# Last tile's operands in three pieces, the first block's norms by halves, and its second-half weights loaded ahead of the merge factors

## The chip, the cores and the metric

The kernel runs on one core of a Trainium2 chip. The metric is the device time of one execution in microseconds (us); three executions are timed and their median is given. One further execution is recorded by the hardware profiler, and every view below is of that one.

## What is computed

One layer of a hybrid decoder for a prompt of 2048 positions and a group of 32 sample rows, in f32:

```python
def _layer_prompt(x, biases, norm1_g, w_in, sgu_ln_g, sgu_ln_b, sgu_w, sgu_b, w_out,
                  norm2_g, w_gate, w_up, w_down):
    q, k, v, u, vg = _project(x, norm1_g, w_in)          # RMSNorm, then one projection
    ...
    att = _merge_branches(outs, lses).reshape(B, S, D_ATT).astype(x.dtype)
    ...
    x = x + jnp.concatenate([att, u * gate], axis=-1) @ w_out
    x = x + _swiglu(x, norm2_g, w_gate, w_up, w_down)
    ...

def _swiglu(x, g, w_gate, w_up, w_down):
    h = _rmsnorm(x, g)
    return (jax.nn.silu(h @ w_gate) * (h @ w_up)) @ w_down
```

D_MODEL is 1024, there are 8 attention heads of 64, and D_FF is 2816, which is 22 slices of 128. After the layer a final RMSNorm gives the result. The change is in the part from the output projection (`w_out`) to the first products with `w_gate` and `w_up`.

## The kernel before

The kernel is one program in four stages: the input projection and the gating unit; attention, head by head; then, for three **blocks** of token tiles (tiles of 128 tokens: 6, 6, and 4 with the sample rows beside them), the output projection with the second norm; and the SwiGLU products of that block. Each operand of a matmul is held as a high and a low part, and each product is three matmuls (high by high, high by low, low by high). The instructions of every engine are issued in the order in which the code is run, so each engine works through its own list in that order and waits at its head. SyncE (SP) issues nearly all DMAs, also in order.

Order in time is written with a clock of **ticks**. `tick()` advances it and runs what `later(n, fn)` has put down for that tick, and only then the matmuls that follow are issued. With `ahead=True` an entry goes before the others of its tick. A tick lies before every four slices of the output projection (12 matmuls) and before every product.

**First block, first half of the columns.** Tile 0 has its first 512 output columns in a PSUM bank already when the block begins. `open_unit` computes those of tiles 1 to 5, in ticks 1 to 10, each into its own bank, by `B.banks = (2, 0, 3, 4, 5, 2)`: tile 5 takes the bank of tile 0 again. `open_end` (an addition on DVE, L1422) empties a bank into the residual `acc`. Between these, `split_cat` makes the high and low parts of the next tile's input. The merged attention of the last head for positions 1024 to 2047 is made here too: `last_half` weights are turned and stored to `f_d` (`turn`, `store`), loaded back spread over the partitions (`merge_load`), multiplied in on POOL (`merge`, in `rest`, L1084 to L1088), and stored to `cat_d` by `merge_store`. The merged values stand in the tiles `obs[h]` (ring `ob`, two buffers) and `o3s[h]` (ring `wide`, two buffers).

**Second half.** `half1_load` loads the eight slices of `w_out` for columns 512 to 1023 into the ring `fraw` (eight buffers), `half1_split` makes their parts: high on ACT, low on POOL (L138). The parts go, two slices at a time, into `wide` (slices 0, 1 and 4, 5; named `woh`) and `ob` (slices 2, 3 and 6, 7; named `wol`), in place of the tiles of heads 6 and 7. `second_phase` then computes the six tiles' second halves and weaves the norms in by `norm2_slot`: slot k ends tile k-1 (`out_end`), sums its squares on ACT, takes the root and its reciprocal, scales it (`norm2_scale`), and turns tile k-2 into operands (`Operands`: 8 transposes on PE, then `first`, `second`, `third`, `last` on ACT, DVE and POOL). In blocks 2 and 3 `first_end` has ended the first half early and summed its squares (`norm2_half`), so that the slot sums 512 columns; in block 1 the slot sums all 1024.

**Products.** `one(u, q)` issues the products q = 0 to 6 of a **unit**, which is one slice of D_FF for some tiles of the block; a product is 12 matmuls into one of four PSUM banks taken in turn. The first slice is cut into two units: tiles 0 to 3 and 4 to 5 in blocks 1 and 2 (256 and 128 columns), two tiles each in block 3 (136 columns each). Before the first product stands slot n, and before product 4 slot n+1, which makes the last tile's operands whole: all of its ACT, DVE and POOL work is issued there. The bank of product 3 is read on DVE in product 4's turn (L1682), and the first product of the second unit, the eighth, takes that bank again. In product 2 the gate's silu runs on ACT (L1701).

Of the kernel before, what the change touches and what calls it, by code (L numbers as in the profile page):

```python
# [65 lines left out]
def hymba_step(ctx: ExitStack, tc: tile.TileContext, A: dict, O: dict):  # L66
# [99 lines left out]
    def zn_tile():  # L166
        return rp.tile([P, 512], F32, name="zn", tag="zn", bufs=3)
# [7 lines left out]
    def raw_tile():  # L175
        return rp.tile([P, 512], F32, name="raw", tag="raw", bufs=RAW)
# [891 lines left out]
    def merge_load(h, ch):  # L1068

        if h < H - 2:  # L1070
            f = pair_tile(F32)
            mf[h, ch] = (f[:, 0], f[:, 1])
            sync.dma_start(f, dap(f_d, h * 2 * T + ch * 512, [[0, P], [T, 2], [1, 512]]))
            return
        mf[h, ch] = (raw_tile(), zn_tile()) if h < H - 1 else (fraw(), fraw())
        for z, t_ in enumerate(mf[h, ch]):
            sync.dma_start(t_, dap(f_d, (h * 2 + z) * T + ch * 512, [[0, P], [1, 512]]))

# [24 lines left out]
    def merge_store(h, c0, c1):  # L1103
        for z in range(2):
            r0 = DA * (z + 1) + h * C
            sync.dma_start(cat_d[r0:r0 + C, c0 * 512:c1 * 512], obs[h][z * C:(z + 1) * C, c0 * 512:c1 * 512])
# [175 lines left out]
    def fraw():  # L1282
        return pool_["fw"].tile([P, 512], F32, name="fr", tag="fr", bufs=8)
# [32 lines left out]
    def later(n, fn, *args, ahead=False):  # L1316
        due[clock[0] + n, not ahead, len(seq)] = (fn, args)
        seq.append(0)

    def tick():  # L1320
        clock[0] += 1
        while due and min(due)[0] <= clock[0]:
            fn, args = due.pop(min(due))
            fn(*args)
# [40 lines left out]
    def split_wo(B, half, s, place, eng_lo=None):  # L1365
        B.wo[half, s] = wh, wl = place(s)
        split_sb(wh, wl, raws.pop(("o", half, s)), eng_lo=eng_lo)
# [69 lines left out]
        newton(r, v)  # L1437
        return r

    def norm2_half(B, i):  # L1440

        B.s1[i] = s1 = fl.tile([P, 4], F32, name="s1", tag="s1", bufs=6)
        act.activation(zn_tile(), B.acc[i][:, 0:512], AF.Square, accum_out=s1[:, 0:1])

    def norm2_square(B, i, junk):

# [204 lines left out]
    def product(B, u, q):  # L1651

        f, a, b = u["f"], u["a"], u["b"]
        n = (b - a) * B.w
        ps = ps_m()[:, 0:n]
        wh, wl = ops[f, q]
        xh, xl = (x[:, a:b, TOK[q]] for x in B.ops)
        out = ps.rearrange("p (i w) -> p i w", w=B.w)
        for k in range(4):
            ks = slice(k * P, (k + 1) * P)  # L1660
            pe.matmul(out, wh[:, ks], xh[:, :, k], start=(k == 0), stop=False)  # L1661
            pe.matmul(out, wh[:, ks], xl[:, :, k], start=False, stop=False)  # L1662
            pe.matmul(out, wl[:, ks], xh[:, :, k], start=False, stop=(k == 3))  # L1663

        rings = ((raw_tile, raw_tile, raw_tile, zn_tile), (zn_tile, zn_tile, zn_tile, raw_tile), (zn_tile, raw_tile, zn_tile, raw_tile))[min(u["n"], 2)]
        if q in (0, 1, 3, 4):
            v = (0, 1, None, 2, 3)[q]
            u["t", v] = rings[v]()[:, 0:n]
        c11, c21, c12, c22 = (u.get(("t", v)) for v in range(4))
        if q == 0:  # L1670
            act.activation(c11, ps, AF.Copy)
        elif q == 1:
            dve.tensor_add(c21, c11, ps)
        elif q == 2:
            dve.tensor_add(c11, c11, ps)
            u["g", 0] = silu_of(u, 0, c11)
        elif q == 3:
            dve.tensor_add(c12, c21, ps)
            u["s1"] = ps
        elif q == 4:  # L1680
            dve.tensor_add(c21, c21, ps)
            dve.tensor_add(c22, c21, u["s1"])  # L1682
        elif q == 5:
            dve.tensor_add(c12, c12, ps)  # L1684
            u["g", 1] = silu_of(u, 1, c12)
        elif q == 6:
            if a == 0:
                B.h[f % FC] = wide_pair("hw") + (hs4[:, f // FC % 2 * FC + f % FC] if B.last else None,)
            lows = hidden(B, u, 1, c22)
            dve.tensor_add(c21, c21, ps)  # L1690
            lows += hidden(B, u, 0, c21)
            for args in lows:
                if f + 1 < NF:
                    later(1, dve.tensor_sub, *args)
                else:
                    dve.tensor_sub(*args)

    def silu_of(u, z, c):

        g = bank(z)[:, 0:c.shape[-1]] if u["f"] else c  # L1700
        act.activation(g, c, AF.Silu)  # L1701
        return g
# [106 lines left out]
    def open_end(B, i):  # L1809
        out_end(B, i, 0, B.open.pop(i))  # L1810
# [39 lines left out]
        for fn, *args in what:  # L1850
            fn(*args)

    def half1_split(B, *ss):
        for s in ss:
            split_wo(B, 1, s, half1_place)

    def half1_load(*ss):
        for s in ss:
            load_wo(1, s, fraw)
# [22 lines left out]
    def second_phase(B, order, after=None):  # L1882

        for k, i in enumerate(order):
            norm2_slot(B, k, order)
            B.half1[i] = ps = ps_o()
            for c in range(2):
                tick()
                out_part(B, i, 1, range(c * 4, c * 4 + 4), ps, c == 0, c == 1)
            if after:  # L1890
                after(i)
        later(1, norm2_slot, B, len(order), order, ahead=True)
        later(5, norm2_slot, B, len(order) + 1, order, ahead=True)

    def first_block(B):

        for i in (1, 2):
            load_cat(B, i, 0, KD, acc_place(2 * i))
        plan.run(10 ** 9)
        split_cat(B, 1)  # L1900
        split_cat(B, 2)
        B.place()
        load_cat(B, 3, 0, KD)
        merge_store(h, 1, 2)
        load_acc(B, 1)
        load_acc(B, 0)
        load_cat(B, 4, 0, KD)
        load_cat(B, 5, 0, KD)
        merge_store(h - 1, 2, 4)
        half1_load(*range(4))  # L1910

        def rest():
            for ch in (2, 3):
                merge(h, ch, pool)
            merge_store(h, 2, 4)
            half1_load(*range(4, KD))
            sync.dma_start(gain[0], dap(A["final_g"], 0, [[0, P], [1, D]]))

        w = last_half["w"]
        for n, what in ((2, [(w.turn, lambda: ps_t(1)), (w.store, zn_tile), (split_cat, B, 3)]),  # L1920
                        (3, [(merge_load, h, 2), (merge_load, h, 3)]),
                        (4, [(split_cat, B, 4), (rest,)]), (5, [(open_end, B, 1)]),
                        (6, [(half1_split, B, 0, 1), (split_cat, B, 5)]), (7, [(open_end, B, 0)]),
                        (8, [(half1_split, B, 2, 3)]), (9, [(half1_split, B, 4, 5), (sources, B, 0, 0, 1, 2, 3)]),
                        (10, [(half1_split, B, 6, 7)]), (11, [(sources, B, 1, 0, 1, 2, 3)])):
            later(n, both, *what)
        for i in (1, 2):
            open_unit(B, i)
        for i in (3, 4, 5):
            open_unit(B, i)  # L1930
        first_operands(B)

        def more_acc(i):
            if i in (1, 2):
                load_acc(B, 2 * i)
                load_acc(B, 2 * i + 1)

        second_phase(B, range(6), more_acc)
# [6 lines left out]
    def next_block(B, downs, finals):  # L1945

        n = len(B.rows)
        order = [n - 1] * B.last + list(range(B.nt))
        B.banks = {i: y for y, i in enumerate(order)}
        B.place()  # L1950
        tiles = [i for i in order if B.rows[i] == P]
        skip = n - len(tiles)
        for j, i in enumerate(tiles):
            if j < 3:
                load_cat(B, i, 0, KD)
            else:
                later(2 * j - 5, load_cat, B, i, 0, KD)
            later(3 + 2 * (j + skip), split_cat, B, i)
        half1_load(*range(4))
        later(3, half1_load, *range(4, KD))  # L1960
        for s in (6, 7):
            later(s - 5, split_wo, B, 0, s, lambda s: op_tile())
        for y, fn in enumerate(finals):
            later(2 + 2 * y, fn)
        for y, i in enumerate(order):
            later(12 + 2 * y, first_end, B, i)
        for y in range(4):
            later(8 + (2 if B.last else 3) * y, half1_split, B, 2 * y, 2 * y + 1)
            later(10 + 3 * y, sources, B, 0, *((2 * y, 2 * y + 1) if y < 3 else (6,)))
        for fn in downs:  # L1970
            fn()
        for i in order:
            open_unit(B, i)
        first_operands(B)
        second_phase(B, order)
# [193 lines left out]
```

## Time and profile before

| | us |
|---|---|
| time, median of 3 executions (lowest to highest) | 2611.22 (2607.18 to 2616.19) |
| the profiled execution's own time | 2606.15 |
| its span, first to last instruction | 2604.4 |
| PE busy with matmuls, share of the span | 2484.0, 95% |
| DVE, ACT, POOL busy | 1411.0, 1220.7, 1373.8 |
| mean granted TensorE clock | 0.979 |

The mean granted clock is the share of full speed that PE was given; a stage with 0.50 does half as much in the same time while PE counts as fully busy. Block 1's part from its first `open_unit` to its first product runs from 941.46 to 1018.47 us of the span; the corresponding first products of blocks 2 and 3 begin at 1620.42 and 2190.95.

### The profile page before, as it was taken

The page shows a single profiled execution, that of the slowest core. Times are in us where ns is not written, and L with a number is a line of the kernel's source. Part 1 is how long each engine was busy: PE and PEld are TensorE (multiplying, and loading weights), DVE is VectorE, ACT ScalarE, POOL GpSimd, SP SyncE. Part 2 cuts the span into 40 slices and gives each one's busy share as a digit, 9 for nine tenths or more (in the row PEclk, how much of TensorE's full clock was granted, in tenths as well). Part 3 has the DMA queues.
Part 4 walks back from the last instruction along what each step waited for, and adds up shares of the span by engine and source line. Part 5 has one row for each costly group of instructions (what it writes and reads, how often), then busy time and mean ns, then how long its engine had stood idle before and what let it go on. Part 6 is the DMA issues. An engine that isn't in the chain of part 4 may idle for free. (4 is left out here: it accounts for less than half of the span.)

```text
span 2604.4 us, 38948 instructions
## 1 busy us (share of the span) xinstructions
PE 2484.0 (95%) x13598; PEld 2192.0 (84%) x13598; DVE 1411.0 (54%) x2772; ACT 1220.7 (47%) x2567; POOL 1373.8 (53%) x1074
## 2 busy tenths in 40 slices
PE   8998899999999889999999999999999999999997
PEld 6777687677988777988989988999999987999996
DVE  3359686345888856444444465444444466444445
ACT  6423334446877746554554545332323335444332
POOL 2035754123576656775766743563544534666663
PEclk9999999999999999999999999999999998999998
DMA  7764853578687664464553564464554643555553
GB/s 244 223 204 146 279 152 126 180 249 271 185 231 222 170 191 159 154 201 143 177 183 129 195 184 144 170 208 156 174 186 147 209 156 118 206 197 199 198 196 110
DMA packets 313408, 479.99 MB, mean 184 GB/s; under 512 B 25841, under 2 KB 178834, under 8 KB 307326
## 3 DMA queue, kind: packets, MB, share of 16 engines
q1 hardware_dynamic: 307740, 468.48, 55.9%
q10 hardware_dynamic: 5474, 9.04, 1.2%
q8 instruction: 108, 1.77, 0.3%
q14 instruction: 86, 0.70, 0.1%
HBM read 381.72 MB, written 165.83 MB: 210 GB/s over the span
## 5 line engine op out<-in xcount | busy, mean ns | idle before, releaser
L1604 POOL TENSOR_TENSOR op<-fr,op 128x512 fp32r<-128x512 f32 x385 | 488.7, 1299 | 299.1 <-ACT op L1600 279.1
L1661 PE MATMUL ps_m<-xh,op 128*128 128x384 f32 (+4 forms) x1932 | 618.6, 320 | 3.7 <-DVE zn L1682 3.7
L1663 PE MATMUL ps_m<-xh,op 128*128 128x384 f32 (+4 forms) x1932 | 618.1, 320 | 0.0
L1662 PE MATMUL ps_m<-xl,op 128*128 128x384 f32 (+4 forms) x1932 | 617.2, 319 | 0.0
L1734 PE MATMUL ps_o<-dw,hw 128*128 128x512 f32 x2040 | 484.0, 392 | 13.1 <-DVE acc L1736 13.1
L1734 PEld LDWEIGHTS ps_o<-dw,hw 128*128 128x128 f32 x2040 | 379.6, 188 | 95.9 <-DVE acc L1736 19.8
L1661 PEld LDWEIGHTS ps_m<-xh,op 128*128 128x128 f32 x1932 | 371.8, 192 | 8.3 <-issue 2.7
L1662 PEld LDWEIGHTS ps_m<-xl,op 128*128 128x128 f32 x1932 | 371.6, 192 | 3.5
L1663 PEld LDWEIGHTS ps_m<-xh,op 128*128 128x128 f32 x1932 | 371.6, 192 | 0.0
L1736 DVE TENSOR_TENSOR acc<-acc,ps_o 128x512 f32<-128x512 f32 (+1 forms) x362 | 247.1, 687 | 213.7 <-PE ps_o L1734 213.7
L1701 ACT ACTIVATE ps_t<-zn 128x384 f32<-128x384 f32 (+1 forms) x126 | 58.3, 463 | 474.0 <-DVE zn L1684 367.8
L1600 ACT ACTIVATE op<-fr 128x512 fp32r<-128x512 f32 x396 | 235.3, 623 | 22.2 <-DMA fr<-ab_d 14.9
L138 POOL TENSOR_TENSOR dw<-fd,dw 128x1024 fp32r<-128x1024 f32 x66 | 158.7, 2405 | 122.1 <-ACT dw L135 122.1
L318 PE MATMUL ps_s<-wh,xh 128*128 128x512 f32 x480 | 197.9, 412 | 6.5 <-ACT xh L135 5.9
L319 PE MATMUL ps_s<-wl,xh 128*128 128x512 f32 x480 | 192.4, 401 | 1.0 <-DVE wl L226 1.0
L320 PE MATMUL ps_s<-wh,xl 128*128 128x512 f32 x480 | 191.6, 399 | 0.0
L1604 POOL TENSOR_TENSOR op<-pair,op 128x512 fp32r<-128x512 f32 x63 | 81.5, 1302 | 117.1 <-ACT op L1600 117.1
L1711 ACT ACTIVATE hw<-ps_t 128x384 fp32r<-128x384 f32 (+1 forms) x126 | 56.0, 453 | 175.3 <-DVE ps_t L1707 174.4
L318 PEld LDWEIGHTS ps_s<-wh,xh 128*128 128x128 f32 x480 | 93.0, 194 | 36.4 <-issue 8.3
L320 PEld LDWEIGHTS ps_s<-wh,xl 128*128 128x128 f32 x480 | 92.8, 193 | 20.6 <-DVE xl L138 0.3
L319 PEld LDWEIGHTS ps_s<-wl,xh 128*128 128x128 f32 x480 | 93.1, 194 | 19.7 <-DVE wl L226 2.2
L611 POOL TENSOR_TENSOR vl<-kv,vh 100x512 fp32r<-100x512 f32 (+1 forms) x32 | 46.0, 1438 | 109.9 <-ACT vh L605 43.9
(484 smaller groups left out, 4776.1 us busy)
## 6 DMA issues: line engine op xcount, KB each, us to landing
fr<-ab_d SPq DMA_DIRECT2D x308, 256.0 KB
fd<-in_w_down_dram SPq DMA_DIRECT2D x66, 512.0 KB
out_ks_dram<-in_cache_k_dram SPq DMA_DIRECT2D x56, 512.0 KB
out_vs_dram<-in_cache_v_dram SPq DMA_DIRECT2D x56, 512.0 KB
ab_d<-fr SPq DMA_DIRECT2D x88, 256.0 KB
raw<-in_w_in_dram SPq DMA_DIRECT2D x72, 256.0 KB
qk_d<-pair SPq DMA_DIRECT2D x64, 256.0 KB
ab_d<-pair SPq DMA_DIRECT2D x63, 256.0 KB
```

The costliest lines, as they stand in the source:

```text
L138: (eng_lo or pool).tensor_sub(lo, src, hi.bitcast(F32))
L318: pe.matmul(o[j], xh[:, k, :], wh, start=(k == 0), stop=False)
L319: pe.matmul(o[j], xh[:, k, :], wl, start=False, stop=False)
L320: pe.matmul(o[j], xl[:, k, :], wh, start=False, stop=(k == KD - 1))
L1600: act.activation(ops[f, j][0], ab[f][j], AF.Copy)
L1604: (pool if f or j in POOL_LOW else dve).tensor_sub(lo_, ab[f][j], hi.bitcast(F32))
L1661: pe.matmul(out, wh[:, ks], xh[:, :, k], start=(k == 0), stop=False)
L1662: pe.matmul(out, wh[:, ks], xl[:, :, k], start=False, stop=False)
L1663: pe.matmul(out, wl[:, ks], xh[:, :, k], start=False, stop=(k == 3))
L1701: act.activation(g, c, AF.Silu)
L1734: pe.matmul(ps[0:nr], l_, r_[:, cs], start=(z == 0 and y == 0), stop=(z == FC - 1 and y == len(pairs) - 1))
L1736: dve.tensor_add(B.acc[i][0:nr, cs], B.acc[i][0:nr, cs], ps[0:nr])
```

## The change

1. **Last tile.** Slot n+1 is replaced by three entries: `Operands` and `first` before product 4, `second` before product 5, `third` and `last` before product 6, in every block. The silu of the first unit's product 2 is issued three ticks later, before product 5 and after `second`.
2. **Norms.** In block 1 the first halves of tiles 0 and 1 are ended and their squares summed in ticks 9 and 7 (`first_half`), where only `open_end` ran in ticks 7 and 5; those of tiles 3 to 5 are ended before the second four slices of their own second half. Tile 2 stays as it was. A square root on one column is issued in tick 10 (`root_ahead`).
3. **Loads.** The merge factors are loaded in tick 2 instead of 3, into `zn` tiles and one `raw` tile instead of four of `fraw`; the storing of head 6's merged values, which stood ahead of tick 1, is issued after them; slices 4 to 7 of the weights are loaded in tick 2 instead of after the last merge's store. `turn` and `store` move from tick 2 to 1.
4. **Splits.** The weights' parts are made in ticks 5, 6, 8 and 9 (were 6, 8, 9 and 10), and the low parts of all slices but 4 and 5 are made on DVE instead of POOL.

```diff
-        mf[h, ch] = (raw_tile(), zn_tile()) if h < H - 1 else (fraw(), fraw())
+        mf[h, ch] = (raw_tile() if h < H - 1 or ch > 2 else zn_tile(), zn_tile())
...
-    def norm2_half(B, i):
+    def norm2_half(B, i, junk=None):
...
-        act.activation(zn_tile(), B.acc[i][:, 0:512], AF.Square, accum_out=s1[:, 0:1])
+        act.activation(zn_tile() if junk is None else junk, B.acc[i][:, 0:512], AF.Square, accum_out=s1[:, 0:1])
...
-            u["g", 0] = silu_of(u, 0, c11)
+
+            def gate():
+                u["g", 0] = silu_of(u, 0, c11)
+
+            if b < B.nt:
+                later(3, gate, ahead=True)
+            else:
+                gate()
...
-    def half1_split(B, *ss):
+    def half1_split(B, eng_lo, *ss):
         for s in ss:
-            split_wo(B, 1, s, half1_place)
+            split_wo(B, 1, s, half1_place, eng_lo)
...
                 tick()
+                if c and k > 2 and i in B.open:
+                    first_end(B, i)
                 out_part(B, i, 1, range(c * 4, c * 4 + 4), ps, c == 0, c == 1)
...
-        later(5, norm2_slot, B, len(order) + 1, order, ahead=True)
+        last = {}
+
+        def last_operands(*steps):
+            if not last:
+                last["x"] = Operands(B, order[-1])
+            for step in steps:
+                getattr(last["x"], step)()
+
+        for n, steps in ((5, ("first",)), (6, ("second",)), (7, ("third", "last"))):
+            later(n, last_operands, *steps, ahead=True)
...
         load_cat(B, 5, 0, KD)
-        merge_store(h - 1, 2, 4)
         half1_load(*range(4))
+
+        def factors():
+            for ch in (2, 3):
+                merge_load(h, ch)
+            merge_store(h - 1, 2, 4)
+            half1_load(*range(4, KD))
 
         def rest():
             for ch in (2, 3):
                 merge(h, ch, pool)
             merge_store(h, 2, 4)
-            half1_load(*range(4, KD))
             sync.dma_start(gain[0], dap(A["final_g"], 0, [[0, P], [1, D]]))
 
+        def first_half(i):
+            open_end(B, i)
+            norm2_half(B, i, B.X[0][:, i, 0:512])
+
+        def root_ahead():
+            t_ = fl.tile([P, 4], F32, name="s1", tag="s1", bufs=6)
+            act.activation(t_[:, 0:1], ident[:, 0:1], AF.Sqrt)
+
         w = last_half["w"]
-        for n, what in ((2, [(w.turn, lambda: ps_t(1)), (w.store, zn_tile), (split_cat, B, 3)]),
-                        (3, [(merge_load, h, 2), (merge_load, h, 3)]),
-                        (4, [(split_cat, B, 4), (rest,)]), (5, [(open_end, B, 1)]),
-                        (6, [(half1_split, B, 0, 1), (split_cat, B, 5)]), (7, [(open_end, B, 0)]),
-                        (8, [(half1_split, B, 2, 3)]), (9, [(half1_split, B, 4, 5), (sources, B, 0, 0, 1, 2, 3)]),
-                        (10, [(half1_split, B, 6, 7)]), (11, [(sources, B, 1, 0, 1, 2, 3)])):
+        for n, what in ((1, [(w.turn, lambda: ps_t(1)), (w.store, zn_tile)]), (2, [(split_cat, B, 3), (factors,)]),
+                        (4, [(split_cat, B, 4), (rest,)]), (5, [(half1_split, B, dve, 0, 1)]),
+                        (6, [(half1_split, B, dve, 2, 3), (split_cat, B, 5)]), (7, [(first_half, 1)]), (8, [(half1_split, B, None, 4, 5)]),
+                        (9, [(half1_split, B, dve, 6, 7), (first_half, 0), (sources, B, 0, 0, 1, 2, 3)]),
+                        (10, [(root_ahead,)]), (11, [(sources, B, 1, 0, 1, 2, 3)])):
             later(n, both, *what)
```

In blocks 2 and 3 the call `half1_split` now passes `None`, which keeps POOL for the low part.

More of the change, by code (lines that the diff above doesn't have):

```diff
@@ L1967, in next_block @@
         for y in range(4):
-            later(8 + (2 if B.last else 3) * y, half1_split, B, 2 * y, 2 * y + 1)
+            later(8 + (2 if B.last else 3) * y, half1_split, B, None, 2 * y, 2 * y + 1)
             later(10 + 3 * y, sources, B, 0, *((2 * y, 2 * y + 1) if y < 3 else (6,)))
```

## The prediction

> **What bounds the kernel now.** PE does, by the page's first part:
>
> ```profile
> PE 2484.0 (95%) x13598; PEld 2192.0 (84%) x13598; DVE 1411.0 (54%) x2772; ACT 1220.7 (47%) x2567; POOL 1373.8 (53%) x1074
> ```
>
> So I look for the time in which it waits or runs slowly around the three places where a block's products begin. First the waits of PE, from 960 to 1050 us (engine and line, what it waited for: us in total, times, longest):
>
> ```profile
> PE ps_t L1474 <- ACT pair L1462: 4.5, 3, 2.1
> PE ps_o L1412 <- POOL woh L138: 2.1, 4, 0.8
> PE ps_m L1661 <- DVE zn L1682: 1.2, 1, 1.2
> ```
>
> The first is the norm of a tile coming late for its transposes, the second the low parts of the second-half weights, the third the bank that the second unit's first product takes over. Next the stretches by windows (length, then PE, PEld, DVE, ACT, POOL busy, granted clock, DMA share, GB/s):
>
> ```profile
> 950.00:960.00 10.00, 10.00 (x46) 8.29 (x45) 3.60 (x6) 3.39 (x6) 0.00 (x0) 1.00 1.09 300
> 963.70:969.10 5.40, 5.40 (x25) 4.50 (x24) 0.00 (x0) 0.00 (x0) 5.32 (x5) 1.00 0.00 0
> 969.10:981.40 12.30, 8.94 (x25) 4.64 (x25) 0.00 (x0) 2.56 (x5) 10.56 (x10) 0.88 0.95 268
> 981.40:1018.50 37.10, 32.60 (x162) 26.50 (x160) 27.55 (x67) 26.33 (x49) 21.95 (x18) 0.99 0.56 181
> 1029.70:1033.10 3.40, 2.26 (x21) 2.29 (x21) 2.78 (x7) 0.83 (x2) 3.31 (x3) 1.00 0.03 9
> 1033.10:1050.20 17.10, 17.10 (x77) 17.10 (x77) 8.20 (x14) 10.45 (x29) 12.72 (x11) 0.50 0.29 106
> 1635.10:1642.20 7.10, 7.10 (x66) 7.10 (x65) 2.64 (x8) 3.92 (x10) 6.23 (x5) 1.00 0.56 184
> 2200.50:2203.90 3.40, 2.04 (x19) 1.93 (x18) 2.15 (x8) 1.82 (x5) 2.55 (x2) 1.00 0.00 0
> 2203.90:2224.40 20.50, 20.50 (x97) 20.50 (x96) 4.09 (x18) 8.19 (x21) 9.40 (x7) 0.50 0.42 129
> ```
>
> Two things stand here. A half tile costs 5.4 us when nothing is late (963.7 to 969.1, tile 5's first half); the next one, tile 0's second half, takes 12.3. And PE counts as fully busy for 17.1 us in block 1 and 20.5 us in block 3 at half the clock. Both stretches begin about 2.3 and 1.2 us after this wait, which all three blocks have:
>
> ```profile
> 1030.84 0.30 PE L1661 MATMUL ps_m<-xh,op 128*128 128x128 f32 x1 [1.19 <-DVE zn L1682]
> ...
> 1632.79 0.30 PE L1661 MATMUL ps_m<-xh,op 128*128 128x128 f32 x1 [1.18 <-DVE zn L1682]
> ...
> 1642.19 0.39 PE L1661 MATMUL ps_m<-xh,op 128*128 128x384 f32 x1
> ...
> 2202.74 0.30 PE L1661 MATMUL ps_m<-xh,op 128*128 128x136 f32 x1 [1.36 <-DVE zn L1682]
> ```
>
> In block 2 the same wait was not followed by a low clock, and its narrow unit (1632.79 to 1642.19) took 9.40 us at 1.00. So a unit of 128 columns does not lower the clock by itself; with the wait in front it did so twice in three. Once low, the clock stayed low until wide products began.
>
> **The last tile in three pieces.** DVE's list in block 1 shows why the bank came late:
>
> ```profile
> 1026.55 0.42 DVE L1490 TENSOR_TENSOR zn<-zn,ps_t 128x256 f32<-128x256 f32 x1 [1.05 <-issue]
> ...
> 1028.00 0.42 DVE L1494 TENSOR_TENSOR zn<-ps_t,zn 128x256 f32<-128x256 f32 x1
> 1029.15 0.69 DVE L1507 TENSOR_TENSOR xl<-ps_t,xh 128x512 fp32r<-128x512 f32 x1 [0.73 <-ACT xh L1499]
> ...
> 1030.27 0.42 DVE L1682 TENSOR_TENSOR zn<-raw,ps_m 128x256 f32<-128x256 f32 x1
> ```
>
> L1682 frees the bank and stands behind the whole of slot n+1. In three pieces only the five subtractions L1490 to L1494 stand ahead, so L1507 and its wait for ACT (from the end of L1494, 1028.42, to near 1029.8, 1.3 us) go: L1682 ends near 1029.4 instead of 1030.69, just before the product was due (1030.84 - 1.19 = 1029.65). The silu, issued later, also lets ACT begin the piece sooner, which adds slack; its table load (1.28 for the root's, below) then lies behind the piece, under products 5 and 6. What is late next: the operands of the second unit's own products, of which POOL's last low part is the latest, several products before its use. I take the three waits as gone: 1.19 + 1.18 + 1.36 = 3.7 us. If the clock stays up it gives 17.1 x 0.5 + 20.5 x 0.5 = 18.8 us; the bounds are nothing and 18.8, and I take 18.8 because block 2's narrow unit, the nearest row, held full clock even with the wait.
>
> The Trainium skill, "TensorE: Matmul & The Clock Gate", section "Why this matters for your kernels", asks only for no PE-idle gaps above about 3 us, since one idle window sends the clock back. By it a wait of 1.2 us costs 1.2 us and its removal 3.7 in all; the trace disagrees in so far as the two low stretches follow such short waits.
>
> A faster narrow unit takes cover from POOL in block 1, which prepares the next slice under it: 12.72 us busy in the 17.1. I put the new wait at 0.8 us, between 0 (ACT's gaps close as PE goes faster) and 4 (12.72 against 9.4 us for the unit is 3.3 short, and a little of the next slice's work).
>
> **Weights, and a new wait.** These rows carry it:
>
> ```profile
> 960.28 0.69 DVE L1403 TENSOR_TENSOR xl<-raw,xh 128x512 fp32r<-128x512 f32 x1
> 960.88 0.68 DVE L1422 TENSOR_TENSOR acc<-acc,ps_m 128x512 f32<-128x512 f32 x1
> ```
> ```profile
> 960.58 1.54 POOL L1084 TENSOR_TENSOR ob<-ob,fr 128x512 f32<-128x512 f32 x1 [27.13 <-DMA fr<-f_d]
> ...
> 967.30 1.29 POOL L1088 TENSOR_TENSOR ob<-ob,o 128x512 f32<-128x512 f32 x1
> ```
> ```profile
> 941.34 1.09 SPq L1106 DMA_DIRECT2D cat_d<-ob  x2
> 942.77 0.87 SPq L1352 DMA_DIRECT2D acc<-in_x_prompt_dram  x2
> 946.71 0.38 SPq L1390 DMA_DIRECT2D xl<-cat_d  x1
> ...
> 954.77 2.90 SPq L1077 DMA_DIRECT2D fr<-f_d  x4
> 968.62 1.09 SPq L1106 DMA_DIRECT2D cat_d<-ob  x2
> ```
> ```profile
> 963.70 0.39 PE L1411 MATMUL ps_m<-op,xh 128*128 128x512 f32 x1
> ```
> ```profile
> 974.24 0.63 ACT L135 ACTIVATE woh<-fr 128x512 fp32r<-128x512 f32 x1 [13.04 <-DMA fr<-in_w_out_dram]
> ```
>
> Before, SP stood at the store of the last merge until POOL was done (967.30 + 1.29 = 968.59) and loaded slices 4 to 7 only then, hence ACT's 13.04 us and most of the 12.3 us. With all eight loaded early and six low parts on DVE (0.69 instead of about 1.3 on POOL, and DVE idle from 961.6 to 981.4), tile 0's second half takes 5.4: 12.3 - 5.4 = 6.9 us gained.
>
> But the order of tick 9 gives it back. Tile 5's first half takes tile 0's bank, and tile 0's `open_end` (960.88 before, in tick 7) now stands behind the low parts of slices 6 and 7 in DVE's list. Those wait for ACT's high parts, which go into head 7's `ob` buffer, and that is read by the last merge's store. PE, in order, waits at 963.70 with everything behind it: the rest of the first half and the whole second half. Step by step: the factors land earlier by the 512 KB of head 6's store that no longer precede them (1.7 us at 300 GB/s), so POOL ends at 968.6 - 1.7 = 966.9. The store then lasts between its issue (1.09) and 946.71 - 941.34 = 5.4 us (the next load of `cat_d` waited for it, in a busy queue); the queue being empty (DMA share 0.00), I take 4.0: 970.9. ACT's 0.63 for slice 6, about 0.5 more for slice 7, DVE's last low part and `open_end`, 0.69 + 0.68, and some 0.3 of hand-overs: 973.7. The wait is 973.7 - 963.7 = 10.0 us (7 to 11.5 by the store). After it PE starts at half clock; the stretch 969.1 to 981.4, which had waits too, lost 12.3 x 0.12 = 1.5, and I take 1.7. Together 11.7 - 6.9 = 4.8 us lost up to the end of tile 0's second half.
>
> Head 6's store, moved behind the factors, holds up slices 2 and 3, and with them `split_cat` of tile 5 on ACT and DVE; the wait above covers that, and without it it would cost 2 to 4 us. The factors wait for `f_d`, which `turn` in tick 1 stores earlier; its source is long ready. On SP the first slice's `sources` still stand behind the last merge's store, but no longer behind four weight loads; their products' preparation is covered by the same wait. `root_ahead` moves a table load into it too.
>
> **Norms.** The rows that price a slot:
>
> ```profile
> 989.37 0.87 PE L1474 MATMUL ps_t<-ident,pair 128*128 128x128 f32 x6 [2.10 <-ACT pair L1462]
> ```
> ```profile
> 985.64 1.28 ACT L1433 ACT_TABLE_LOAD   x1
> ...
> 998.05 1.06 ACT L1455 ACTIVATE xh<-acc 128x1024 fp32r<-128x1024 f32 x1
> ...
> 1614.52 0.63 ACT L1450 ACTIVATE xh<-acc 128x512 fp32r<-128x512 f32 x1
> ```
>
> Tile 0's wait of 2.10 goes: its chain loses the table load (1.28) and 0.43 of squares, and POOL's work on the first weights, behind which its end stood, is done during the new wait. Of the other two (4.5 - 2.1 = 2.4), tile 2's keeps its full square and one later is shorter by about 0.4, since DVE's list is as long as before. I take 2.5 us gained, between 1.5 and 4.5.
>
> **The sum**, against the profiled execution's own 2606.15 us (span 2604.4 and 1.75 around it): 2606.15 - 3.7 - 18.8 + 0.8 + 4.8 - 2.5 = 2586.8. The median of the runs, 2611.22, lies 5.1 above that execution; since which waits lower the clock differs from place to place, I expect part of the difference to remain and add half: 2589.
>
> **Rivals.**
> - *No wait at tile 5* (the store or a buffer is free earlier than I read): 2589 - 11.7 + 3 for tile 5's inputs that then come late = 2580. For it: the low parts of slices 6 and 7 were not waiting for that store before. Against: the buffer's order in the ring. 0.14.
> - *The low clock is not the short wait's doing.* Then 18.8 stays: 2608, no change that can be told. For it: a wait of 1.18 without it, in block 2. Against: block 2's narrow unit at 1.00, so the narrowness does not do it either. 0.10. The Trainium skill's rule on gaps, weighed above, would have it so.
> - *The bank is still late*, as five subtractions stay ahead of L1682 with only 0.3 us to spare by the first estimate: 2589 + 3.7 + 18.8 = 2611.5, no change. 0.07.
> - *Slower: the wait moves into the narrow unit.* POOL's low part for product 4 of the second unit comes a piece later; if it ends after that product is due, the gap stands amid 128-column products, where few columns flow in any case, and all three blocks go low: block 2 loses its 9.4 us, the 22.5 do not come back: 2589 + 22.5 + 9.4 = 2621. It decides once the piece is over 3 us later than I count. 0.07.
> - *As forecast*: 0.62.
>
> **Numbers.** A measurement here tells 0.3%, 7.8 us, from no change: faster is below 2603.4, slower above 2619.1. Faster: 0.62 + 0.14, less a little for a longer wait, 0.75; same: 0.18; slower: 0.07. The range reaches from the first rival's 2580, less 5 for the norm's and the median's bounds (2575), to the second's 2608 (2609).
>
> **What would show it.** Right: no wait of L1661 for L1682 in the three blocks, clock 1.00 in both narrow units; PE idle 7 to 11.5 us ahead of tile 5's first half, ended by DVE's L1422, with a low clock after it; no wait for `woh` or `wol` in tile 0's second half; one wait of about 1 us left for L1462; block 1's first product 1 to 4 us later than 1018.47. Wrong: tile 5 starting at 963.7, or a clock of 0.50 in a narrow unit.

## The result, and the profile after

The changed kernel takes 2600.19 us (median of 7 runs, 2593.92 to 2604.76) against 2611.22 us: a ratio of 0.9956, 95% interval 0.9938 to 0.9975, so 11.5 us gained, between 6.5 and 16.2. The prediction of 2589 had the sign and the range, and nearly twice the gain. Its profiled execution took 2604.76 us (span 2602.7), the slowest of the seven.

First the waits of PE, from 940 to 1110 us (engine and line, what it waited for: us in total, times, longest). Lines after the change are numbered higher: L1741 and L1743 were L1734 and L1736, L1708 was L1701, L1689 does what L1682 did. L1661 to L1663 are the three matmuls of a product, L1604 is the subtraction on POOL that makes a low part of the products' operands, L1741 the matmuls with `w_down`, and L1743 the addition on DVE that empties their bank.

```profile
PE ps_m L1411 <- DVE acc L1422: 11.6, 1, 11.6
PE ps_t L1474 <- ACT pair L1462: 3.0, 2, 2.3
PE ps_o L1741 <- DVE acc L1743: 3.0, 1, 3.0
PE ps_m L1663 <- POOL op L1604: 2.0, 1, 2.0
```

The waits for the bank (L1661) and for the weights (`woh`, `wol`) are gone, as forecast, and the wait at tile 5 is there: 11.6 us. New are the last two rows, inside block 1's products. Now the stretches (length, then PE, PEld, DVE, ACT, POOL busy, granted clock, DMA share, GB/s):

```profile
981.00:988.00 7.00, 6.98 (x24) 5.67 (x25) 1.51 (x1) 2.63 (x5) 4.28 (x4) 0.78 1.18 314
988.00:993.40 5.40, 5.40 (x25) 4.49 (x24) 0.00 (x0) 0.00 (x0) 0.00 (x0) 1.00 0.22 82
1041.25:1050.60 9.35, 9.35 (x87) 9.35 (x85) 6.48 (x11) 5.48 (x16) 7.74 (x6) 1.00 0.23 85
1050.60:1068.70 18.10, 16.09 (x87) 15.78 (x86) 6.54 (x11) 10.25 (x27) 17.10 (x14) 0.93 0.34 108
2209.80:2219.20 9.40, 9.40 (x87) 9.40 (x85) 6.69 (x14) 6.07 (x17) 6.10 (x5) 1.00 0.34 112
```

Tile 5's first half runs partly cold (7.0 us instead of 5.4), tile 0's second half takes the 5.4 us of an undisturbed one, and the narrow units of blocks 1 and 3 take 9.35 and 9.40 us at full clock. Before, the narrow unit and slice 1 of block 1 looked like this:

```profile
1030.80:1046.70 15.90, 15.86 (x84) 15.89 (x85) 7.36 (x13) 9.51 (x28) 11.52 (x10) 0.57 0.27 100
1046.70:1063.00 16.30, 16.30 (x87) 16.30 (x87) 6.50 (x11) 7.56 (x13) 16.22 (x12) 0.89 0.52 168
```

So 6.5 us are won in the narrow unit and 1.8 lost in the slice after it. To see where the rest went, the first product of each block, first before, then after:

```profile
1018.47 0.37 PE L1661 MATMUL ps_m<-xh,op 128*128 128x256 f32 x1
1620.42 0.36 PE L1661 MATMUL ps_m<-xh,op 128*128 128x256 f32 x1
2190.95 0.31 PE L1661 MATMUL ps_m<-xh,op 128*128 128x136 f32 x1
```
```profile
1030.23 0.37 PE L1661 MATMUL ps_m<-xh,op 128*128 128x256 f32 x1
1630.26 0.37 PE L1661 MATMUL ps_m<-xh,op 128*128 128x256 f32 x1
2199.50 0.31 PE L1661 MATMUL ps_m<-xh,op 128*128 128x136 f32 x1
```

Before, PE reaches tile 5 at 963.70; after, it is ready at 981.02 - 11.61 = 969.41. That 5.7 us lies in code ahead of the change, where the granted clock differs from one execution to the next. The rest by stages:

| stage | forecast | before | after | difference |
|---|---|---|---|---|
| PE ready for tile 5 to block 1's first product | +4.8 - 2.5 = +2.3 | 54.8 | 60.8 | +6.0 |
| block 1's first product to block 2's | -1.2 - 8.5 + 0.8 = -8.9 | 602.0 | 600.0 | -1.9 |
| block 2's to block 3's | -1.2 | 570.5 | 569.2 | -1.3 |
| block 3's to the end of the span | -1.4 - 10.2 = -11.6 | 413.5 | 403.2 | -10.3 |

The sum is -7.5 against a forecast of -19.4 (2606.15 to 2586.8). Blocks 2 and 3 came as forecast; block 1 did not, ahead of its products and in them.

### The profile page after: what moved, and what is told of

It reads as the page before. It is cut to its first block, busy times and chain, and to the rows that moved or that the text cites. A ratio compares the mean times of both kernels' runs of the same rounds, so it can differ in the third digit from the quotient of the medians.

```text
span 2602.7 us, 38973 instructions
## 1 busy us (share of the span) xinstructions
PE 2472.9 (95%) x13598; PEld 2183.8 (84%) x13598; DVE 1426.8 (55%) x2783; ACT 1222.2 (47%) x2578; POOL 1367.1 (53%) x1068
## 4 chain that ended last, share of the span: by engine, by line
PE 35%; issue 8%; POOL 8%; DMA 5%; ACT 2%; DVE 1%; SPq 1%; POOLq 0%; ACTq 0%; DVEq 0%
PE ps_o L1741 11%; PE ps_m L1663 7%; PE ps_m L1661 7%; PE ps_m L1662 7%; POOL op L1604 3%; DMA ab_d<-pair 2%; ACT fr L1572 1%; POOL dw L138 1%; POOL pair L1584 1%; POOL pair L1593 1%; POOL fr L1587 1%; DMA out_yp_dram<-acc 1%; POOL pair L1590 1%; PE ps_o L1411 0%; PE ps_o L1412 0%
## 5 line engine op out<-in xcount | busy, mean ns | idle before, releaser
L1604 POOL TENSOR_TENSOR op<-fr,op 128x512 fp32r<-128x512 f32 x385 | 488.3, 1297 | 286.4 <-ACT op L1600 276.3
L1663 PE MATMUL ps_m<-xh,op 128*128 128x384 f32 (+4 forms) x1932 | 611.7, 317 | 2.3 <-POOL op L1604 2.3
L1661 PE MATMUL ps_m<-xh,op 128*128 128x384 f32 (+4 forms) x1932 | 611.6, 317 | 0.0
L1662 PE MATMUL ps_m<-xl,op 128*128 128x384 f32 (+4 forms) x1932 | 610.6, 316 | 0.0
L1741 PE MATMUL ps_o<-dw,hw 128*128 128x512 f32 x2040 | 485.8, 393 | 15.0 <-DVE acc L1743 15.0
L1741 PEld LDWEIGHTS ps_o<-dw,hw 128*128 128x128 f32 x2040 | 380.7, 188 | 98.4 <-DVE acc L1743 22.1
L1661 PEld LDWEIGHTS ps_m<-xh,op 128*128 128x128 f32 x1932 | 364.7, 189 | 4.0
L1662 PEld LDWEIGHTS ps_m<-xl,op 128*128 128x128 f32 x1932 | 364.4, 189 | 3.5
L1663 PEld LDWEIGHTS ps_m<-xh,op 128*128 128x128 f32 x1932 | 364.4, 189 | 2.8 <-POOL op L1604 2.8
L1743 DVE TENSOR_TENSOR acc<-acc,ps_o 128x512 f32<-128x512 f32 (+1 forms) x362 | 247.1, 687 | 214.7 <-PE ps_o L1741 214.6
L1708 ACT ACTIVATE ps_t<-zn 128x384 f32<-128x384 f32 (+1 forms) x126 | 58.3, 463 | 464.9 <-DVE zn L1691 365.3
L1604 POOL TENSOR_TENSOR op<-pair,op 128x512 fp32r<-128x512 f32 x63 | 81.4, 1301 | 116.7 <-ACT op L1600 116.7
L1718 ACT ACTIVATE hw<-ps_t 128x384 fp32r<-128x384 f32 (+1 forms) x126 | 56.1, 453 | 175.2 <-DVE ps_t L1714 174.2
L135 ACT ACTIVATE dw<-fd 128x1024 fp32r<-128x1024 f32 x66 | 69.8, 1057 | 72.5 <-DMA fd<-in_w_down_dram 72.5
```

Source lines behind the costliest of these rows:

```text
L135: act.activation(hi, src, AF.Copy)
L1604: (pool if f or j in POOL_LOW else dve).tensor_sub(lo_, ab[f][j], hi.bitcast(F32))
L1741: pe.matmul(ps[0:nr], l_, r_[:, cs], start=(z == 0 and y == 0), stop=(z == FC - 1 and y == len(pairs) - 1))
L1743: dve.tensor_add(B.acc[i][0:nr, cs], B.acc[i][0:nr, cs], ps[0:nr])
```

## The experiments

All are timed beside the kernel before on the same chip; us are medians, ratios are to the kernel before with their 95% intervals, and a ratio is turned into us by 2611.

**The pieces alone.** The kernel before with `last_operands` and the late gate:

```
-        later(5, norm2_slot, B, len(order) + 1, order, ahead=True)
+        for n, steps in ((5, ("first",)), (6, ("second",)), (7, ("third", "last"))):
+            later(n, last_operands, *steps, ahead=True)
```

> The kernel before with only the last tile's operands in three pieces (and the gate's silu later). Theory P (in block 1 POOL, ACT behind it and DVE behind that pace the products up to about 1090 us, so what PE wins in block 1's narrow unit is given back there; blocks 2 and 3 keep theirs): 0 to 2 us from block 1, about 1.9 from block 2 and 11 from block 3, so 2611 - 13 = 2598, and waits for L1604 or L1743 in block 1's products. Rival F (the terms of the prediction: 3.7 + 18.8 - 0.8): 2589.

2590.4 us, 0.9936 (0.9916 to 0.9955): -16.7 us, between the two, and the interval holds both. By the ratios the pieces alone come out 5 us ahead of the whole change; the intervals overlap.

**Everything but the pieces.** The other half: the changed kernel with the old line in place of the new ones.

> The changed kernel with the last tile's operands in one slot again and the silu in product 2: the loads, splits and norms of the change alone. Theory P: block 1's first product about 6 us later than before (11.6 of wait at tile 5, less 5.5 in tile 0's second half, norms nearly nothing when a cold window falls on them), of which about 4.6 remains at 1250 us; low clock in the narrow units again: 2611 + 4.6 = 2616. Rival F: + 4.8 - 2.5 = 2613.

2617.58 us, 1.0023 (1.0008 to 1.0038): 6.0 us slower than before. The two halves add up: -16.7 + 6.0 = -10.7 against -11.5. The bank's wait is back in all three blocks; the clock fell in block 3's narrow unit, and not in those of blocks 1 and 2 (here and below, windows):

```profile
1039.05 0.30 PE L1661 MATMUL ps_m<-xh,op 128*128 128x128 f32 x1 [1.18 <-DVE zn L1682]
...
2210.75 0.30 PE L1661 MATMUL ps_m<-xh,op 128*128 128x136 f32 x1 [1.36 <-DVE zn L1682]
```
```profile
1039.00:1048.50 9.50, 9.45 (x85) 9.48 (x85) 7.00 (x12) 4.85 (x14) 7.46 (x7) 1.00 0.23 84
...
2210.80:2226.50 15.70, 15.70 (x84) 15.70 (x85) 3.54 (x15) 5.48 (x16) 7.56 (x7) 0.57 0.44 151
```

**Pieces in blocks 2 and 3 only.**

```
+        for n, steps in (((5, ("first", "second", "third", "last")),) if B.b0 == 0 else
+                         ((5, ("first",)), (6, ("second",)), (7, ("third", "last")))):
```

> The changed kernel with the last tile's operands undivided in block 1 only (and the silu in product 2 there). Theory P: the 1.2 us wait and a low clock come back in block 1's narrow unit, POOL then waits less and PE no more for POOL after it; block 1 ends within 3 us of the changed kernel's: 2600 to 2603, verdict same. Rival F: 1.2 + 8.6 lost: 2610.

2600.72 us, 0.9965 (0.9952 to 0.9978), against 0.9956 for the change: in block 1 the pieces are worth 2.3 us by these ratios, which is within the intervals. Blocks 2 and 3 give 15 us (1.0023 to 0.9965). In the profile the bank's wait is back in block 1 (1.18 us), but the low clock that both theories counted on is not: the narrow unit took 9.4 us at 1.00.

**What the wait does to the clock.** The addition that frees the bank repeated on DVE, so that the wait grows:

```
-            dve.tensor_add(c22, c21, u["s1"])
+            for _ in range(1 if u["n"] else (17 if B.last else 11)):
+                dve.tensor_add(c22, c21, u["s1"])
```

> The changed kernel, with the addition that empties the bank which the second unit takes over (L1689) repeated on DVE, the same values each time, so that the second unit's first product waits about 2.4 us for the bank in all three blocks. Theory C (a gap in front of the 128- and 136-column products is what lowers the clock, and these products then keep it low): clock 0.50 in the narrow units of blocks 2 and 3, 2 x (2.4 + 9) = 23 us, and 2 to 5 in block 1: 2625 to 2628. Rival: the low clock has another cause; 2.4 us a block, 2605 to 2607.

2632.98 us, 1.0091 (1.0072 to 1.0109). The waits came out at 3.52, 3.53 and 4.33 us, longer than meant, and all three narrow units ran cold to their ends:

```profile
1039.90:1057.20 17.30, 17.30 (x84) 17.30 (x85) 7.49 (x14) 10.03 (x29) 12.63 (x10) 0.52 0.24 91
1644.70:1662.70 18.00, 17.95 (x84) 17.98 (x85) 5.58 (x14) 5.98 (x14) 8.49 (x7) 0.50 0.48 161
2228.90:2246.90 18.00, 17.97 (x85) 18.00 (x85) 5.17 (x16) 6.07 (x17) 8.51 (x7) 0.50 0.39 132
```

By the ratios this is 35 us more than the changed kernel, of which the waits themselves are 11.4. Over the three blocks of all 14 profiled executions: without a wait in front none of 32 narrow units ran cold; with 1.2 to 1.4 us 3 of 7 did (the kernel before in blocks 1 and 3, the one without pieces in block 3); with 3.5 to 4.3 us 3 of 3. So the wait is the cause. What decides after a short one is not shown: block 1 fell once in three, block 2 never in two, and block 3, where the unit ahead is 136 columns wide too, both times.

**The wait at tile 5.** Its chain in the changed kernel:

```profile
961.48 1.24 SPq L1106 DMA_DIRECT2D cat_d<-ob  x2
968.40 1.15 ACT L135 ACTIVATE wol<-fr 128x512 fp32r<-128x512 f32 x2 [5.49 <-DMA cat_d<-ob]
971.32 1.59 POOL L1088 TENSOR_TENSOR ob<-ob,o 128x512 f32<-128x512 f32 x1
972.93 1.09 SPq L1106 DMA_DIRECT2D cat_d<-ob  x2
975.47 0.63 ACT L1443 ACTIVATE xh<-acc 128x512 fp32r<-128x512 f32 x1 [1.36 <-DVE acc L1422]
976.10 1.13 ACT L135 ACTIVATE woh<-fr 128x512 fp32r<-128x512 f32 x2
977.14 1.13 ACT L135 ACTIVATE wol<-fr 128x512 fp32r<-128x512 f32 x2
977.84 2.44 DVE L138 TENSOR_TENSOR wol<-fr,wol 128x512 fp32r<-128x512 f32 x2 [2.40 <-ACT wol L135]
980.20 0.68 DVE L1422 TENSOR_TENSOR acc<-acc,ps_m 128x512 f32<-128x512 f32 x1
981.02 0.77 PE L1411 MATMUL ps_m<-op,xh 128*128 128x512 f32 x1 [11.61 <-DVE acc L1422]
```

The end is the forecast one: high parts of slices 6 and 7, low parts, `open_end`, PE. What comes before it is not. ACT did not wait at 977.14 for the last merge's store (972.93): it came there straight from the parts of slices 4 and 5 (976.10), and it was late because of head 6's store (961.48), which held up the parts of slices 2 and 3 until 968.40, with tile 5's split and tile 1's end behind them. In the reordered kernel below, ACT does wait for the last merge's store, and that store took 3.9 us from its issue (966.55):

```profile
970.48 1.15 ACT L135 ACTIVATE wol<-fr 128x512 fp32r<-128x512 f32 x2 [2.77 <-DMA cat_d<-ob]
```

If it took as long here, it was done near 976.9 (an estimate), some 0.3 us before ACT came to it. To test the end of the chain, tick 9 was turned round:

```
-(9, [(half1_split, B, dve, 6, 7), (first_half, 0), (sources, B, 0, 0, 1, 2, 3)])
+(9, [(first_half, 0), (half1_split, B, dve, 6, 7), (sources, B, 0, 0, 1, 2, 3)])
```

> The changed kernel, with tile 0's first half ended (open_end, its squares) ahead of the split of slices 6 and 7 in tick 9. If DVE's order made the wait of 11.6 us at tile 5, it goes, and 1 to 3 us of wait for slice 6 or 7 in tile 0's second half comes: block 1's first product 8 to 10 us earlier than in the changed kernel, and since POOL's list of block 1 starts as much earlier, the end too: 2600 - 9 = 2591. Rival: the last merge's store holds the weights' and the first slice's loads anyway, and POOL's list starts no earlier: under 3 us, 2597 to 2600.

2593.37 us, 0.9943 (0.9923 to 0.9964). The wait did not go; it fell to 6.7, and what is left is the other store's:

```profile
953.58 1.09 SPq L1106 DMA_DIRECT2D cat_d<-ob  x2
960.55 1.15 ACT L135 ACTIVATE wol<-fr 128x512 fp32r<-128x512 f32 x2 [5.69 <-DMA fr<-in_w_out_dram]
961.22 2.48 DVE L138 TENSOR_TENSOR wol<-fr,wol 128x512 fp32r<-128x512 f32 x2 [5.64 <-ACT wol L135]
967.26 0.68 DVE L1422 TENSOR_TENSOR acc<-acc,ps_m 128x512 f32<-128x512 f32 x1
968.09 0.77 PE L1411 MATMUL ps_m<-op,xh 128*128 128x512 f32 x1 [6.70 <-ACT xh L1443]
```

This is head 6's store, which the change moved behind the factors: ACT's parts of slices 2 and 3 begin 7 us after its issue, with tile 5's split and tile 0's end queued behind them. (The trace names a weight load at 960.55, where that of the changed kernel names the store at 968.40, and ACT's L1443 at 968.09. PE starts 0.15 us after DVE's L1422 ends, 967.94: of several semaphores the trace names one.) So both splits were moved behind the tiles:

```
+(6, [(split_cat, B, 5)]), (7, [(first_half, 1), (first_half, 0)]),
+(8, [(half1_split, B, dve, 2, 3), (half1_split, B, None, 4, 5)]),
+(9, [(half1_split, B, dve, 6, 7), (sources, B, 0, 0, 1, 2, 3)]),
```

> The changed kernel with, in block 1's first half, tile 5's split and both ends of tiles 1 and 0 ahead of the splits of slices 2 to 7 (tick 6: split_cat of 5; tick 7: tiles 1 and 0 ended; tick 8: slices 2 to 5; tick 9: slices 6 and 7). If in the kernel with only tile 0 ended first (2593.4) the 6.7 us at tile 5 came from head 6's store, behind which slices 2 and 3, then tile 5's split, then tile 0's end stood, the wait goes; 0.5 to 2 us for slices 6 and 7 come in tile 0's second half: block 1's first product 9 to 11 us earlier than in the changed kernel, 2588. Rival: tile 5's own input lands that late; the wait stays at 4 to 7 us, 2593.

2589.68 us, 0.9924 (0.9906 to 0.9943), and PE waits nowhere in tile 5's first half nor in tile 0's second. Not all of it was kept. The norm of tile 0 now waits:

```profile
PE ps_t L1474 <- ACT pair L1462: 6.9, 2, 4.7
```
```profile
977.65 1.51 DVE L1584 TENSOR_TENSOR raw<-fr 128x512 f32<-128x512 f32 x1 [5.16 <-POOL fr L1569]
979.09 0.67 DVE L1422 TENSOR_TENSOR acc<-acc,ps_o 128x512 f32<-128x512 f32 x1
```

Tile 0's end stands behind the first sum of slice 0, which waits for the slice's loads, which stand behind the last merge's store on SP. With slice 0's preparation a tick later (`later(1 + y + (B.b0 == 0), prepare, B, 0, y)`):

> The kernel with tiles 5, 1 and 0 ahead of the splits (2589.7), and slice 0's preparation in block 1 one tick later, so that tile 0's end on DVE no longer stands behind the first sum of slice 0 (L1584), which waits for POOL and the first slice's loads. If that order made the 4.7 us of wait for L1462, it goes: 2585. Rival: the preparation, a tick later, is late for the first products, or the norm's own chain is as long: 2589 to 2591.

2586.95 us, 0.9907 (0.989 to 0.9924), clear of the changed kernel's interval and so better than both. Of the 4.7, 1.5 is left, and a wait of 4.0 came at a later tile. By the ratios the step won 4.4 us, but the intervals of the two kernels overlap, so it isn't shown to pay by itself.

**The norms.** The changed kernel with the loads, the stores and the splits as before:

> The changed kernel with the loads, the order of the stores and the splits of the second-half weights as before: pieces and norms alone. Against the kernel with the pieces alone (2590.4) it prices the norms. Theory N (the norms give next to nothing: one long wait for L1462 stays, 36.8 us from tile 1's second half to the first product in the changed kernel against 37.1 before and 38.0 with the pieces alone): 0 to 1.5 us earlier, 2589 to 2590. Rival F (the prediction's term): 2.5 earlier, 2588, with one wait of about 1 us for L1462. Either way about 10 under the changed kernel.

2593.01 us, 0.9935 (0.9917 to 0.9953), against 0.9936 for the pieces alone: nothing. The waits for L1462 between 985 us and the first product, here and then with the pieces alone, moved and did not shrink:

```profile
PE ps_t L1474 <- ACT pair L1462: 5.2, 4, 2.2
```
```profile
PE ps_t L1474 <- ACT pair L1462: 4.2, 2, 2.8
```

**Why block 1 keeps nothing.** The first idea was POOL's list. Three sums of slice 1 went to DVE, and the third piece was issued with the second:

```
+((5, ("first",)), (6, ("second", "third")), (7, ("last",)))
+        d, eng = ab[f], pool if f > 1 or (f and j == 5) else dve
```

> The changed kernel with 5.9 us less on POOL's list between the last slot and slice 1 of block 1: three sums of slice 1 (L1584, L1587, L1590) on DVE, and the third piece's parts issued with the second, ahead of the silu and its table load on ACT. Theory P (block 1's first products are paced by POOL's list): the waits for L1604 (2.0) and L1743 (3.0) go or shrink to under 2 together, and block 2's first product comes 4 to 6 us sooner after block 1's (599.8 in the undisturbed traces): 2595. Rival: they wait for the DMAs of the slice's sources; both waits stay, 2600.

2600.77 us, 0.9966 (0.9952 to 0.9981): nothing, and both waits stood to the tenth of a microsecond.

```profile
PE ps_o L1741 <- DVE acc L1743: 3.0, 1, 3.0
PE ps_m L1663 <- POOL op L1604: 2.0, 1, 2.0
```

What I had taken away, POOL spent waiting for ACT's high parts (3.20, 2.49 and 0.86 us). So I looked at ACT's list in the changed kernel:

```profile
1049.34 2.43 ACT L1572 ACTIVATE fr<-fr,g2c 128x128 f32<-128x128 f32 x8
1051.68 0.62 ACT L1600 ACTIVATE op<-fr 128x512 fp32r<-128x512 f32 x1
1052.20 2.44 ACT L1572 ACTIVATE fr<-fr,g2c 128x128 f32<-128x128 f32 x8
...
1054.75 0.62 ACT L1600 ACTIVATE op<-pair 128x512 fp32r<-128x512 f32 x1
```

Sixteen multiplications by the gain, for slice 2, stand ahead of high parts that slice 1 needs now. Sixteen more, for slice 3, begin at 1074.70 and 1078.31, ahead of two instructions (L1718 and L1671) for which DVE waits 5.0 and 2.6 us before it comes to L1743. Without these 32:

```
-        for k in range(4 * (f > 1)):
+        for k in range(4 * (f > 3)):
```

> The changed kernel without the 32 multiplications by the gain on ACT for slices 2 and 3 of block 1 (left out: those two slices lack their gain), 9.8 us less on ACT's list, in front of the high parts for which POOL's low parts wait. Theory P2 (from the narrow unit on, ACT's list and POOL's behind it, in their order, set when slice 1's last parts come): of the 2.0 us for L1604 and the 3.0 for L1743 at most 1 is left, 2593 to 2595. Rival: POOL's own list, or the slices' DMAs, set it: at least 3 us of the two waits stay, 2599 to 2600.

2589.32 us, 0.992 (0.9907 to 0.9933), 9.4 under the changed kernel by the ratios. The wait for L1743 is gone, the other is halved:

```profile
PE ps_m L1663 <- POOL op L1604: 1.0, 1, 1.0
```
```profile
1022.96 0.36 PE L1661 MATMUL ps_m<-xh,op 128*128 128x256 f32 x1
...
1615.54 0.36 PE L1661 MATMUL ps_m<-xh,op 128*128 128x256 f32 x1
```

From block 1's first product to block 2's it is now 592.6 us instead of 600.0: 4.0 us of waits, and the cold stretches that followed them. So ACT's gains set the pace of block 1's first slices. The 1.0 us that is left is POOL's own: in this kernel its list has no gap from 1035.45 to 1077.45 us.

**A version that keeps the work.** On top of the reordered kernel with the later preparation, the gain of slices 2 and 3 on DVE, all of it or every other quarter:

```
+        if f in (2, 3) and q % 2 == 0:
+            w4 = w_.rearrange("p (k c) -> p k c", k=4)
+            dve.tensor_mul(w4, w4, g2c[:, k0:k0 + 4].unsqueeze(2).broadcast_to([P, 4, P]))
```

> The kernel with the reordered first half and slice 0's preparation a tick later (2587), with the gain of slices 2 and 3 of block 1 multiplied in on DVE: 8 additions to DVE's list of about 0.7 us in place of 32 on ACT of 0.305 (9.8 us). If ACT's list sets block 1's pace, the waits for L1604 and L1743 fall from 5.0 to about 1 as in the kernel without the gains, and block 2 starts some 7 us sooner after block 1: 2580. Rival: the four on DVE in the narrow unit hold up the emptying of the banks there, PE waits over 1.5 us amid narrow products and the clock falls: 2587 to 2592.

> The same with every other gain on DVE (4 there, 16 left on ACT, 4.9 us less on ACT): about half, 2583 to 2584, if ACT's list sets the pace; the risk to the banks is half as large. Rival: 2587.

All on DVE: 2585.5 us, 0.9912 (0.989 to 0.9933); a multiplication took 0.8 to 2.6 us on DVE (median 1.8) where 0.7 was expected, DVE stood 7.2 us at one whose load had not landed, with the silu's products behind it, and PE waited 2.4 us for those in turn. Half on DVE: 2583.06 us, 0.9901 (0.9881 to 0.9921), the lowest median here, by the ratios 14 under the changed kernel and 26 under the one before; its interval overlaps that of the kernel without this last step (0.9907), so the step itself isn't shown to pay. Two waits remain among its block 1's products (the lines stand three further on in this kernel):

```profile
PE ps_o L1744 <- DVE acc L1746: 2.1, 2, 1.3
PE ps_m L1666 <- POOL op L1607: 1.9, 1, 1.9
```

## Why the prediction was right, and where it was wrong

**Right: the bank and the clock.** The three waits went, both narrow units kept the full clock, and the longer wait brought the low clock into all three blocks. Block 3 gave 10.3 us of a forecast 11.6. Blocks 2 and 3 together gave 15 us by runs and 11.6 in the pair of profiles; the difference may be executions of the kernel before in which block 2 ran cold too, which its one profile does not show.

The rival that took its cue from the Trainium skill ("TensorE: Matmul & The Clock Gate", section "Why this matters for your kernels": no idle gaps above about 3 us) falls in part: waits of 1.2 to 1.4 us were followed by a low clock in 3 of 7 cases, and without one in none of 32, though at 3.5 us and more it was 3 of 3. The same page, in "A second HAM failure mode: psum-queue depth-cycling", tells of a clock that falls because TensorE idles briefly and often between groups of matmuls while it cycles through banks, so there too short idling counts. No run shows that very case: here a single wait stood ahead of each cold unit.

**Wrong: "A faster narrow unit takes cover from POOL in block 1 ... I put the new wait at 0.8 us, between 0 ... and 4".** This is the term that cost the forecast most. PE waited 2.0 us for POOL's L1604 and 3.0 for DVE's L1743, and in the profiled execution the clock fell after each. Of a forecast 8.9 us from block 1's first product to block 2's, 1.9 stayed. The effect was named, and its engine was wrong for the larger part: I compared POOL's busy time with the unit's length, and the list that set the pace was ACT's, with 9.8 us of gains ahead of high parts that were due. Taking POOL's work away changed nothing; taking ACT's away gave 7.4 us and left 1.0 us of wait to POOL. It fits that block 1's cold narrow unit cost little before the change: with the same wait a warm narrow unit (599.6 us to block 2's first product in the kernel without pieces, 601.1 in the one with pieces in blocks 2 and 3 only) and the cold one of the kernel before (602.0) differ by 0.8 to 2.4 us, not by 6.5.

**Right at its end, wrong above it: tile 5.** The wait came where I had it, 11.6 us against 10.0 (7 to 11.5), with 1.6 for the cold start against 1.7, and tile 0's second half at 5.4 as said: 6.3 lost up to there against 4.8. The step that failed is that of head 6's store, "the wait above covers that". The last merge ended 972.91 - 969.41 = 3.5 us after PE was ready (4.9 before, so 1.4 sooner where I had 1.7), and its store took 3.9 us where I had 4.0, but ACT came to slices 6 and 7 only after that, held up by head 6's store: uncovered, in the kernel with tile 0's end first, this costs 6.7 us, not 2 to 4. That the size still came out near the forecast is in part luck: the two paths ended within about 0.3 us of each other. Most of what was short is the last leg: I had 2.8 us from ACT's start on slice 6 to PE, and it took 3.9, because DVE's two subtractions took 2.44 us with POOL at work beside them.

**Wrong: the norms.** Forecast 2.5 us, between 1.5 and 4.5; worth nothing by runs, and 0.3 in the trace (6.3 lost at the end of tile 0's second half, 6.0 at the first product). The wait of 2.1 for tile 0 went and one of 2.3 came further on, with a cold stretch behind it. "One wait of about 1 us left" was the step that failed: I followed the first tile's chain and took the later ones as they were.

**The median.** I added half of the 5.1 us by which the runs lay above the profiled execution. With 7 runs the kernel before stayed at 2611.22, so that its profiled execution was a quick one, and that of the changed kernel the slowest of its seven; the ratio of the runs, not the pair of traces, is the measure.

## What to carry to other kernels

Before a low clock is priced as a loss, ask whether the other engines would have kept up with the full one: list by list, in issue order, from the first operand that is due, and not by an engine's busy share. A wait of PE is worth most where the products behind it are narrow, since these did not bring the clock back within 16 to 18 us, while the 512-column products behind the 11.6 us at tile 5 ran at full speed again after 3.1 us. And when a store's source is also the next writer's buffer, every instruction queued behind that writer waits for the store: moving loads ahead of a store moves this wait, and an order that puts the work that PE needs ahead of the writer removes it.

## What the hardware showed beside

DVE slows down beside POOL. Two subtractions of 128x512 took 1.31 us with POOL idle and, in the same execution (the kernel with tile 0's end first), 2.48 in the row at 961.22 above, with POOL at work:

```profile
954.26 1.31 DVE L138 TENSOR_TENSOR woh<-fr,woh 128x512 fp32r<-128x512 f32 x2 [1.79 <-ACT woh L135]
```
```profile
961.43 1.71 POOL L1086 TENSOR_TENSOR o<-o,zn 128x512 f32<-128x512 f32 x1
```

The Trainium skill, "GPSIMD Engine Reference", section "1. Specifications", has the two share their SBUF interfaces, with contention for DVE instructions of two SBUF inputs; the rows agree, POOL's own going from 1.29 to 1.71.

The stage ahead of the change, the same code in all kernels here, had a granted clock of 0.97 in the profiled execution before and 0.96 after:

```profile
20.00:940.00 920.00, 851.35 (x4639) 704.39 (x4639) 601.26 (x1185) 498.75 (x1004) 422.66 (x376) 0.97 0.67 203
```
```profile
20.00:940.00 920.00, 849.86 (x4607) 704.03 (x4605) 596.54 (x1173) 498.50 (x1003) 422.63 (x376) 0.96 0.68 202
```

This may be why the executions of one kernel spread over 10 us and more. Of 59 executions of the kernel before that were timed beside the experiments, the ten quickest had a mean clock of 0.978 to 0.982 and the ten slowest one of 0.974 to 0.979. That it is the short waits which lower it at other places each time is not shown for this stage.
